# A gate folded into the down weights, three tiles' sums gated early into the residual, and a last quarter normalised on other engines

## The chip, the cores and the metric

The kernel runs on one core of a Trainium2 chip. The metric is the device time of one execution in microseconds (us); for the kernel before it is 829.94 us, the median of three runs (828.57 to 830.37). Engines are named as in the profile: PE is TensorE's matmuls, DVE is VectorE, ACT is ScalarE, POOL is GpSimd, SP is the queue that issues the DMAs.

## What is computed

One layer of a diffusion backbone over 512 tokens of width 1024. Only its last part bears on the change: the gated MLP with a 3x3 depthwise convolution, its down-projection, the gated residual and the last layer norm.

```python
def _conv_ffn(u, rows, cols, w_up, conv_w, conv_b, w_down):
    ...
    a, b = jnp.split(h.reshape(B, L, 2 * D_FF), 2, axis=-1)
    return (jax.nn.gelu(a) * b) @ w_down

def _layer(...):
    ...
    u2 = _modulate(x, sh2, sc2)
    x = _post_norm(DEEPNORM_ALPHA * x + g2 * _conv_ffn(u2, rows, GRID_W, w_up, conv_w, conv_b, w_down),
                   ln2_g, ln2_b)
```

`g2` is a row of 1024 numbers, one for each output column, so it may be multiplied into the sum after the matmuls or into the columns of `w_down` before them. The inner width is 2816, that is 22 tiles of 128 rows of `w_down`.

## The kernel before

**Precision by three matmuls.** Every float32 product is made of three matmuls (`mm3`, lines 92 to 95). A weight tile is split into a rounded half `hi`, which ACT casts (line 88, or 1009 in `spare_split`), and a rest `lo`, which a subtraction makes on DVE or POOL (line 83). Its raw tile (`raw4`, six buffers) comes by one DMA of 512 KB.

**Convolution stage** (lines 1069 to 1097). For each of 44 feature tiles PE makes one PSUM bank (24 matmuls); ACT starts the accumulator and two scaled copies (lines 1078, 1081); POOL adds those two taps (line 996) and makes the `lo` of a later weight tile (line 83); DVE adds six taps (line 998), three for this tile and three for the one before, and a gate product (line 1057) or a `lo` of the activations (line 83). In these loops the order on each engine is as the code says.

**Down stage** (lines 1106 to 1144). The 512 tokens are four blocks, the 1024 output columns two halves, so eight PSUM banks hold all the sums. For each weight tile f (0 to 17 here) all eight banks take three matmuls. `down_prep(f)` loads and splits tile f, with the subtraction on DVE and POOL in turn (`alt`). Only the SP queue's order is fixed there; a scheduler places the instructions of the other engines, and may put them among those of the convolution stage. The last four tiles (18 to 21) are split into kept tiles `lasth`, `lastl`; ACT scales the residual `x1` by ALPHA (line 1141).

**End** (lines 1145 to 1225). For each half of each block the four last tiles are multiplied (`piece`); then DVE multiplies the sum by g2 (line 1152), adds the residual (1153) and takes statistics (1166). The last block's second half is worked in two quarters. The norm is finished on three engines: `finish_pool` (ACT, then two POOL operations), `finish_act` with `centred` (DVE, ACT, one POOL operation), and two DVE operations for the last block. `store` sends each half out.

Of the kernel before, what the change touches and what calls it, by code (L numbers as in the profile page):

```python
# [21 lines left out]
NTB = SEQ // P  # L22
# [23 lines left out]
def layer_kernel(ctx: ExitStack, tc: tile.TileContext, a: dict):  # L46
    nc = tc.nc
    act, dve, pool, pe, dma = nc.scalar, nc.vector, nc.gpsimd, nc.tensor, nc.sync
# [14 lines left out]
    def raw4(shape=(P, D)):  # L63
        return sb.tile(list(shape), F32, tag="raw", bufs=6, name=nm("raw"))
# [38 lines left out]
    part = keep("part", [P, 2, 16])  # L103
# [234 lines left out]
    wh, wl = (sb.tile([P, NF0], F32R, tag=t, bufs=2, name=nm(t)) for t in ("hi", "lo"))  # L338
# [9 lines left out]
    ready = wh, wl  # L348
# [473 lines left out]
    lng = load(row(), a["ln1_g"].broadcast_to([P, D]))  # L822
    lnb = load(row(), a["ln1_b"].broadcast_to([P, D]))
# [3 lines left out]
    x1 = slot(4, [P, NTB, D])  # L827
# [241 lines left out]
    for i in range(2 * NFF):  # L1069
        ps = up_mm(i)  # L1070
# [19 lines left out]
        f = i // 2 - 1  # L1090
# [22 lines left out]
    def down_mm(ps, tb, f, wh, wl, cs, first, last):  # L1113
        ts_ = slice(tb * P, (tb + 1) * P)
        mm3(ps, acts[f // 8][:, f % 8, ts_], acts[3 + f // 8][:, f % 8, ts_], wh[:, cs], wl[:, cs], first, last)

    def down(tb, f, wh, wl):
        for hf, cs in enumerate(HALVES):
            split_end = f == N_FRONT - 1 and hf == 1 and tb == NTB - 1
            down_mm(banks[tb][hf], tb, f, wh, wl, cs, f == 0, split_end)  # L1120

    for w, f in ((down0, 0), (down1, 1)):
        for tb in range(NTB - 1):
            down(tb, f, *w)
    ready = down2
    for w, f in ((down0, 0), (down1, 1)):
        down(NTB - 1, f, *w)
    lasth = slot(1, [P, NFF - N_FRONT, D], F32R)
    lastl = slot(8, [P, NFF - N_FRONT, D], F32R)
    for f in range(2, N_FRONT):  # L1130
        w = ready
        if f + 1 < N_FRONT:
            ready = down_prep(f + 1, alt())
        for tb in range(NTB):
            down(tb, f, *w)
        if f >= N_FRONT - 8 and f % 2 == 0:
            i = (f - N_FRONT + 8) // 2
            raw = load(raw4(), a["w_down"][N_FRONT + i])
            act.copy(lasth[:, i, :], raw)
            sub(dve, lastl[:, i, :], raw, lasth[:, i, :].bitcast(F32))  # L1140
            tc.keep_in_program_order(act.activation(x1[:, i, :], x1[:, i, :], AF.Copy, scale=ALPHA))
    part = banks[NTB - 1][1]
    dve.tensor_tensor(part, part, g2[:, HALVES[1]], ALU.mult)
    dve.tensor_tensor(x1[:, NTB - 1, HALVES[1]], part, x1[:, NTB - 1, HALVES[1]], ALU.add)
    ordered(*ORDT)

    QUARTERS = tuple(slice(i, i + CTX) for i in range(0, D, CTX))
    end = NTB - 1
    st, mean, scale, parts = {}, {}, {}, {}

    def residual(tb, ps, cs):
# [28 lines left out]
    def centred(tb):  # L1180
        for ps, cs in parts[tb]:
            dve.scalar_tensor_tensor(ps, ps, mean[tb], lng[:, cs], ALU.subtract, ALU.mult)

    def finish_pool(tb):
        nmr = small([P, 1])
        dve.tensor_scalar(nmr, mean[tb], scale[tb], -1.0, ALU.mult, ALU.mult)
        for ps, cs in parts[tb]:
            act.activation(x1[:, tb, cs], ps, AF.Identity, bias=nmr, scale=scale[tb])
        for ps, cs in parts[tb]:
# [4 lines left out]
            yield

    def finish_act(tb):
        for ps, cs in parts[tb]:
            z = x1[:, tb, cs]
            act.activation(z, ps, AF.Copy, scale=scale[tb])
            pool.tensor_tensor(z, z, lnb[:, cs], ALU.add)  # L1200
            store(tb, cs)

    for tb in range(end):
        piece(tb, HALVES[0], 0, 2)
        if tb == 1:
            weave(finish_pool(0))
        elif tb:
            finish_act(tb - 1)
        piece(tb, HALVES[1], 1, 2)
        block_scale(tb)  # L1210
        if tb == 1:
            centred(tb)
    piece(end, HALVES[0], 0, 3)
    late = finish_pool(end - 1)
    next(late)
    piece(end, QUARTERS[2], 1, 3)
    piece(end, QUARTERS[3], 2, 3)
    block_scale(end)
    centred(end)
    for i, (ps, cs) in enumerate(parts[end]):  # L1220
        dve.scalar_tensor_tensor(x1[:, end, cs], ps, scale[end], lnb[:, cs], ALU.mult, ALU.add)
        if i != 1:
            store(end, HALVES[min(i, 1)])
        weave(late)
# [75 lines left out]
```

## Time and profile before

| what | us |
|---|---|
| median of three runs | 829.94 |
| the profiled execution | 828.57 |
| its span, first to last instruction | 826.8 |
| PE busy | 801.3 (97%) |
| DVE busy | 537.5 (65%) |
| POOL busy | 401.6 (49%) |
| ACT busy | 365.1 (44%) |

The profiled execution took 828.57 us, of which 1.77 us lie around the span of 826.8 us. Busy shares are means over the whole span; where an engine waits, and for whom, is read from the engines' timelines, in us from the span's start. The convolution stage ends and the down stage begins near 697 us; the last matmul starts at 816.70 us.

### The profile page before, as it was taken

What the parts mean: (1) busy time and instruction counts of PE and PEld (TensorE: products, weight loads), DVE (VectorE), ACT (ScalarE), POOL (GpSimd) and SP (SyncE); (2) the same over time, 40 slices, a digit from 0 to 9 for tenths busy, and PEclk for the clock granted to TensorE, in tenths of its full rate; (3) what the DMA queues carried; (4) which work ended last, traced back from release to release, by engine and by line L of the source; (5) the groups of instructions that cost most, each with busy time, mean ns of one, the idle gap of its engine ahead of it and who ended that gap; (6) DMA issues with size and microseconds to landing.
All of it is one profiled execution on the core that took longest, in us unless ns stands there. A gap on an engine that the chain in (4) does not pass through costs nothing.

```text
span 826.8 us, 10600 instructions
## 1 busy us (share of the span) xinstructions
PE 801.3 (97%) x3865; PEld 668.9 (81%) x3865; DVE 537.5 (65%) x1040; ACT 365.1 (44%) x579; POOL 401.6 (49%) x295
## 2 busy tenths in 40 slices
PE   6989999999999999999999999999999999999995
PEld 4768877888888888888788998888888888888884
DVE  7947789884267773333667579887778877522147
ACT  4644526221454343323325476665566556233101
POOL 3754360021443242104624779988888888321106
PEclk9999999999999999999999999999999999999998
DMA  9950359973220006460504512322232222343002
GB/s 342 405 199 1 140 205 328 324 259 120 75 77 26 1 2 253 133 201 9 205 21 185 192 38 85 117 83 97 103 103 102 83 97 102 102 153 102 1 1 101
DMA packets 34356, 106.94 MB, mean 129 GB/s; under 512 B 4592, under 2 KB 5376, under 8 KB 34304
## 3 DMA queue, kind: packets, MB, share of 16 engines
q1 hardware_dynamic: 34304, 106.27, 36.7%
q8 instruction: 30, 0.49, 0.2%
q14 instruction: 22, 0.18, 0.1%
HBM read 104.14 MB, written 2.11 MB: 129 GB/s over the span
## 4 chain that ended last, share of the span: by engine, by line
PE 87%; DVE 5%; POOL 2%; ACT 2%; issue 2%; DMA 1%; POOLq 0%; SPq 0%; DVEq 0%; ACTq 0%
PE ps L95 26%; PE ps L94 26%; PE ps L93 26%; PE ps L356 3%; PE ps L674 1%; PE ps L644 1%; PE ps L675 1%; POOL S L83 1%; DVE raw L205 1%; DVE S L258 1%; DVE lo L83 1%; PE ps L636 1%; DMA S<-in_x 1%; PE ps L641 1%; POOL lo L83 1%
## 5 line engine op out<-in xcount | busy, mean ns | idle before, releaser
L95 PE MATMUL ps<-S,lo 128*128 128x512 f32 (+1 forms) x560 | 216.4, 388 | 4.2 <-POOL lo L83 3.2
L93 PE MATMUL ps<-S,hi 128*128 128x512 f32 (+1 forms) x560 | 218.2, 390 | 1.0 <-ACT hi L88 1.0
L94 PE MATMUL ps<-S,hi 128*128 128x512 f32 (+1 forms) x560 | 217.1, 388 | 0.0
L83 POOL TENSOR_TENSOR lo<-raw,hi 128x1024 fp32r<-128x1024 f32 (+3 forms) x61 | 141.2, 2317 | 154.6 <-ACT hi L88 152.0
L998 DVE SCALAR_TENSOR_TENSOR t<-ps,convw,t 128x441 f32<-128x441 f32 (+1 forms) x258 | 163.8, 690 | 45.3 <-POOL t L996 45.1
L88 ACT CAST hi<-raw 128x1024 fp32r<-128x1024 f32 (+1 forms) x96 | 99.3, 1035 | 176.1 <-PE ps L95 61.3
L95 PEld LDWEIGHTS ps<-S,lo 128*128 128x128 f32 x560 | 105.6, 189 | 26.9 <-POOL lo L83 4.0
L93 PEld LDWEIGHTS ps<-S,hi 128*128 128x128 f32 x560 | 105.5, 188 | 22.6 <-ACT hi L88 1.5
L94 PEld LDWEIGHTS ps<-S,hi 128*128 128x128 f32 x560 | 105.6, 189 | 21.2
L996 POOL TENSOR_TENSOR t<-t,t 128x448 f32<-128x448 f32 x88 | 101.9, 1158 | 34.4 <-ACT t L1081 31.0
L95 PE MATMUL ps<-S,S 128*128 128x512 f32 (+1 forms) x308 | 112.2, 364 | 0.0
L94 PE MATMUL ps<-S,S 128*128 128x512 f32 (+1 forms) x308 | 112.2, 364 | 0.0
L93 PE MATMUL ps<-S,S 128*128 128x512 f32 (+1 forms) x308 | 111.4, 365 | 0.0
L83 DVE TENSOR_TENSOR lo<-raw,hi 128x1024 fp32r<-128x1024 f32 x37 | 47.2, 1276 | 68.0 <-ACT hi L88 68.0
L94 PE MATMUL ps<-lo,S 128*128 128x512 f32 x208 | 81.0, 390 | 0.0
L95 PE MATMUL ps<-hi,S 128*128 128x512 f32 x208 | 80.8, 389 | 0.0
L93 PE MATMUL ps<-hi,S 128*128 128x512 f32 x208 | 77.2, 391 | 1.6 <-ACT S L546 1.0
L83 POOL TENSOR_TENSOR S<-raw,S 128x1024 fp32r<-128x1024 f32 x21 | 50.6, 2410 | 38.9 <-ACT S L765 23.5
L1078 ACT ACTIVATE t<-ps,convb,convw 128x512 f32<-128x512 f32 x43 | 33.6, 781 | 75.2 <-PE ps L95 75.2
L93 PEld LDWEIGHTS ps<-S,S 128*128 128x128 f32 x308 | 58.1, 189 | 9.2
L94 PEld LDWEIGHTS ps<-S,S 128*128 128x128 f32 x308 | 58.1, 189 | 9.2
L95 PEld LDWEIGHTS ps<-S,S 128*128 128x128 f32 x308 | 58.1, 189 | 9.1
(219 smaller groups left out, 1065.3 us busy)
## 6 DMA issues: line engine op xcount, KB each, us to landing
raw<-in_w_up SPq DMA_DIRECT2D x44, 512.0 KB, 3.3
raw<-in_wada SPq DMA_DIRECT2D x32, 512.0 KB, 5.3
raw<-in_w_down SPq DMA_DIRECT2D x22, 512.0 KB, 3.3
S<-in_wada SPq DMA_DIRECT2D x16, 512.0 KB, 9.6
raw<-in_w_v SPq DMA_DIRECT2D x16, 256.0 KB, 4.5
raw<-in_w_ga SPq DMA_DIRECT2D x8, 512.0 KB, 4.3
raw<-in_w_gb SPq DMA_DIRECT2D x8, 512.0 KB, 3.3
raw<-in_w_br SPq DMA_DIRECT2D x8, 512.0 KB, 4.0
```

The source lines that it names most:

```text
L83: eng.tensor_tensor(out, x, y, ALU.subtract)
L88: act.copy(hi, raw)
L93: pe.matmul(out, lhsT=sh, rhs=mh, start=first, stop=False)
L94: pe.matmul(out, lhsT=sh, rhs=ml, start=False, stop=False)
L95: pe.matmul(out, lhsT=sl, rhs=mh, start=False, stop=last)
L205: dve.scalar_tensor_tensor(out_junk, raw, 1.0, silu_c, ALU.mult, ALU.mult, accum_out=mod[:, j:j + 1])
L258: dve.scalar_tensor_tensor(junk[:, cs], ada_slot(j)[:, cs], 1.0, silu_h[hf], ALU.mult, ALU.mult, accum_out=dst[:, j:j + 1])
L356: pe.matmul(g0[f], lhsT=w[:, f * P:(f + 1) * P], rhs=m[:, kt, :], start=kt == 0 and i == 0, stop=kt == NKT - 1 and i == 2)
L636: pe.matmul(score[h + i][:, ns], lhsT=kT[half_rows, t, ns], rhs=qT[half_rows, t, ns], start=True, stop=True)
L996: pool.tensor_tensor(o, o, i, ALU.add)
L998: dve.scalar_tensor_tensor(o, i, w, o, ALU.mult, ALU.add)
L1078: act.activation(acc, src, AF.Identity, bias=convb[:, i:i + 1], scale=convw[:, i, 4:5])
```

## The change

- Every weight tile of the down stage from f = 3 on, the four kept ones among them, is multiplied by g2 on DVE right after its load (`gated_down`, a product of two tiles of 128x1024 in SBUF); all subtractions of the tiles 3 to 17 are on POOL.
- Tiles 0 to 2 are not multiplied beforehand. Their sums are closed in the eight banks, DVE multiplies each bank by g2 and adds it to ALPHA times the residual (two operations of 128x512 for each bank), and the banks begin anew with tile 3. ACT's four scalings of `x1` are gone.
- At the end DVE no longer multiplies by g2. Blocks 0 to 2 are all finished the same way (DVE, ACT, one POOL operation), and of the last block the last quarter goes over ACT and POOL, the rest over DVE.

```diff
     def down_prep(f, eng):
+        return (split if f % 3 else spare_split)(gated_down(f), (P, D), eng)
+
+    def gated_down(f):
         raw = load(raw4(), a["w_down"][f])
-        return (split if f % 3 else spare_split)(raw, (P, D), eng)
+        dve.tensor_tensor(raw, raw, g2, ALU.mult)
+        return raw
...
+    for blocks, tiles in (((0, 1), (0, 1)), ((0, 1), (2,)), ((2, 3), (0,)), ((2, 3), (1,)), ((2, 3), (2,))):
+        for f in tiles:
+            for tb in blocks:
+                down(tb, f, plain[f], f == N_PLAIN - 1)
+        if tiles == (2,):
+            for tb in blocks:
+                for hf, cs in enumerate(HALVES):
+                    ps = banks[tb][hf]
+                    dve.tensor_tensor(ps, ps, g2[:, cs], ALU.mult)
+                    dve.scalar_tensor_tensor(x1[:, tb, cs], x1[:, tb, cs], ALPHA, ps, ALU.mult, ALU.add)
+    ready = down_prep(N_PLAIN, pool)
...
-            ready = down_prep(f + 1, alt())
+            ready = down_prep(f + 1, pool)
...
-            tc.keep_in_program_order(act.activation(x1[:, i, :], x1[:, i, :], AF.Copy, scale=ALPHA))
-    dve.tensor_tensor(part, part, g2[:, HALVES[1]], ALU.mult)
...
-        dve.tensor_tensor(ps, ps, g2[:, cs], ALU.mult)
-        dve.tensor_tensor(ps, ps, x1[:, tb, cs], ALU.add)
+        dve.tensor_tensor(ps, ps, x1[:, tb, cs], ALU.add)
...
     block_scale(end)
+    centred(end, 0)
+    nmr = small([P, 1])
+    dve.tensor_scalar(nmr, mean[end], scale[end], -1.0, ALU.mult, ALU.mult)
+    ps, cs = parts[end][2]
+    z = x1[:, end, cs]
+    act.activation(z, ps, AF.Identity, bias=nmr, scale=scale[end])
+    pool.tensor_tensor(z, z, lng[:, cs], ALU.mult)
+    pool.tensor_tensor(z, z, lnb[:, cs], ALU.add)
+    scaled(end, 0)
+    store(end, HALVES[0])
+    centred(end, 1)
+    scaled(end, 1)
+    store(end, HALVES[1])
```

The change in the order of instructions is shown at three places. In the names `t_...` are accumulators of the convolution, `ps_...` PSUM banks, `raw_...` raw weight tiles, `row_6082` is g2 and `S_520` is the residual `x1`; line 1029 of the changed kernel is the g2 product, lines 1138 and 1139 are the two operations on a bank.

DVE, in the convolution stage, from the gate product of feature tiles 36 and 37 to the first taps of tile 39 (before):

```order
L1057 TENSOR_TENSOR ps_5825<-ps_5825,t_845_5766 128x512
L998 SCALAR_TENSOR_TENSOR t_852_5813<-ps_5788,convw,t_852_5813 128x8x63
L998 SCALAR_TENSOR_TENSOR t_858_5859<-ps_5834,convw,t_858_5859 128x7x63
L998 SCALAR_TENSOR_TENSOR t_852_5813<-ps_5788,convw,t_852_5813 128x7x63
L998 SCALAR_TENSOR_TENSOR t_858_5859<-ps_5834,convw,t_858_5859 128x7x63
```

and after:

```order
L1062 TENSOR_TENSOR ps_5825<-ps_5825,t_845_5766 128x512
L998 SCALAR_TENSOR_TENSOR t_852_5813<-ps_5788,convw,t_852_5813 128x8x63
L1029 TENSOR_TENSOR raw_6184<-raw_6184,row_6082 128x1024
L998 SCALAR_TENSOR_TENSOR t_858_5859<-ps_5834,convw,t_858_5859 128x7x63
L998 SCALAR_TENSOR_TENSOR t_852_5813<-ps_5788,convw,t_852_5813 128x7x63
L998 SCALAR_TENSOR_TENSOR t_858_5859<-ps_5834,convw,t_858_5859 128x7x63
```

The g2 product of weight tile 3 now stands ahead of the first tap of feature tile 39, where DVE waited for POOL; those of tiles 4 to 7 stand ahead of the first taps of feature tiles 40 to 43 in the same way.

DVE, from the last taps of the convolution into the down stage (before):

```order
L998 SCALAR_TENSOR_TENSOR t_887_6049<-t_886_6047,convw,t_887_6049 128x8x63
L998 SCALAR_TENSOR_TENSOR t_887_6049<-t_886_6047,convw,t_887_6049 128x7x63 x2
L1057 TENSOR_TENSOR t_893_6071<-t_893_6071,t_887_6049 128x512
L83 TENSOR_TENSOR S_603_4032<-t_893_6071,S_600_4029 128x512
L83 TENSOR_TENSOR S_603_4032<-raw_6146,S_600_4029 128x1024
```

and after:

```order
L998 SCALAR_TENSOR_TENSOR t_887_6049<-t_886_6047,convw,t_887_6049 128x8x63
L998 SCALAR_TENSOR_TENSOR t_887_6049<-t_886_6047,convw,t_887_6049 128x7x63
L1029 TENSOR_TENSOR raw_6313<-raw_6313,row_6082 128x1024
L998 SCALAR_TENSOR_TENSOR t_887_6049<-t_886_6047,convw,t_887_6049 128x7x63
L1138 TENSOR_TENSOR ps_6088<-ps_6088,row_6082 128x512
L1138 TENSOR_TENSOR ps_6089<-ps_6089,row_6082 128x512
L1062 TENSOR_TENSOR t_893_6071<-t_893_6071,t_887_6049 128x512
L1138 TENSOR_TENSOR ps_6090<-ps_6090,row_6082 128x512
L1138 TENSOR_TENSOR ps_6091<-ps_6091,row_6082 128x512
L1139 SCALAR_TENSOR_TENSOR S_520_3425<-S_520_3425,ps_6088 128x512
L1139 SCALAR_TENSOR_TENSOR S_520_3425<-S_520_3425,ps_6089 128x512
L1138 TENSOR_TENSOR ps_6092<-ps_6092,row_6082 128x512
```

The g2 product of weight tile 8 and the operations on the banks now stand between the last taps and the last gate product; the first bank (`ps_6088`) is read for the last time by the first row of line 1139. PE writes that bank again with the first matmul of tile 3, in both kernels the 73rd of the down stage, so it follows that row now.

POOL, at the end of the program (before):

```order
L1174 TENSOR_TENSOR sm_6758<-sm_6758,neg_half 128x1
L1191 TENSOR_TENSOR S_520_3425<-S_520_3425,row_6084 128x512
L1192 TENSOR_TENSOR S_520_3425<-S_520_3425,row_6086 128x512
L1174 TENSOR_TENSOR sm_6818<-sm_6818,neg_half 128x1
L1191 TENSOR_TENSOR S_520_3425<-S_520_3425,row_6084 128x512
L1192 TENSOR_TENSOR S_520_3425<-S_520_3425,row_6086 128x512
```

and after:

```order
L1180 TENSOR_TENSOR sm_6780<-sm_6780,neg_half 128x1
L1202 TENSOR_TENSOR S_520_3425<-S_520_3425,row_6086 128x512 x2
L1180 TENSOR_TENSOR sm_6838<-sm_6838,neg_half 128x1
L1213 TENSOR_TENSOR S_520_3425<-S_520_3425,row_6084 128x256
L1214 TENSOR_TENSOR S_520_3425<-S_520_3425,row_6086 128x256
```

Of block 2 POOL has two operations instead of four, both ahead of the last block's square root (the 128x1 row); behind it stand two of 256 columns instead of two of 512.

## Rows read from the trace of the kernel before

**Rows 1.** The page: chain that ended last by engine; then a DMA issue, us to landing

```profile
PE 87%; DVE 5%; POOL 2%; ACT 2%; issue 2%; DMA 1%; POOLq 0%; SPq 0%; DVEq 0%; ACTq 0%
...
raw<-in_w_down SPq DMA_DIRECT2D x22, 512.0 KB, 3.3
```

**Rows 2.** PE's timeline: start, us, engine, line, operation; two places of the down stage

```profile
713.31 1.98 PE L93 MATMUL ps<-S,S 128*128 128x512 f32 x8
...
816.70 0.28 PE L95 MATMUL ps<-S,S 128*128 128x256 f32 x1
```

**Rows 3.** DVE's timeline, end of the convolution stage, and one later row

```profile
679.30 3.08 DVE L998 SCALAR_TENSOR_TENSOR t<-ps,convw,t 128x441 f32<-128x441 f32 x5 [1.06 <-POOL t L996]
...
682.89 0.73 DVE L998 SCALAR_TENSOR_TENSOR t<-ps,convw,t 128x504 f32<-128x504 f32 x1
...
695.66 3.08 DVE L998 SCALAR_TENSOR_TENSOR t<-ps,convw,t 128x441 f32<-128x441 f32 x5 [1.18 <-POOL t L996]
...
701.86 2.79 DVE L998 SCALAR_TENSOR_TENSOR t<-t,convw,t 128x441 f32<-128x441 f32 x1 [1.88 <-POOL t L996]
...
707.59 2.16 DVE L998 SCALAR_TENSOR_TENSOR t<-t,convw,t 128x504 f32<-128x504 f32 x3
...
726.89 1.23 DVE L83 TENSOR_TENSOR S<-raw,S 128x1024 fp32r<-128x1024 f32 x1 [0.15 <-ACT S L1139]
```

**Rows 4.** POOL's timeline, near 105 us

```profile
105.02 2.15 POOL L480 TENSOR_TENSOR t<-t,t 128x512 f32<-128x512 f32 x1
107.25 2.16 POOL L83 TENSOR_TENSOR t<-t,t 128x512 f32<-128x512 f32 x1
```

**Rows 5.** DVE's timeline, same stretch

```profile
105.96 2.30 DVE L83 TENSOR_TENSOR lo<-raw,hi 128x1024 fp32r<-128x1024 f32 x1
```

**Rows 6.** POOL's timeline, end of the convolution stage

```profile
679.20 2.43 POOL L83 TENSOR_TENSOR lo<-raw,hi 128x1024 fp32r<-128x1024 f32 x1
...
701.79 2.39 POOL L83 TENSOR_TENSOR lo<-raw,hi 128x1024 fp32r<-128x1024 f32 x1
```

**Rows 7.** Busy us in a stretch: PE, PEld, DVE, ACT, POOL; clock, DMA, GB/s

```profile
600.00:700.00 100.00, 100.00 (x443) 82.81 (x442) 79.93 (x130) 62.52 (x95) 84.92 (x56) 1.00 0.29 98
```

**Rows 8.** SP's timeline: the load of down weight tile 3

```profile
676.26 0.33 SPq L98 DMA_DIRECT2D raw<-in_w_down  x1
```

**Rows 9.** ACT's timeline: first cast of the down stage; two finishing operations

```profile
711.11 1.05 ACT L1009 CAST S<-raw 128x1024 fp32r<-128x1024 f32 x1
...
816.69 1.45 ACT L1188 ACTIVATE S<-ps,sm,sm 128x512 f32<-128x512 f32 x2 [3.17 <-DVE sm L1186]
```

**Rows 10.** DVE's timeline, end of the program

```profile
811.27 0.70 DVE L1166 BATCH_NORM_STATS2 t<-ps 128x6 f32<-128x512 f32 x1
811.88 0.68 DVE L1152 TENSOR_TENSOR ps<-ps,row 128x512 f32<-128x512 f32 x1
...
817.84 0.42 DVE L1152 TENSOR_TENSOR ps<-ps,row 128x256 f32<-128x256 f32 x1
...
819.50 0.15 DVE L1173 TENSOR_SCALAR sm<-sm 128x1 f32<-128x1 f32 x1
```

**Rows 11.** POOL's timeline, end of the program

```profile
820.10 0.55 POOL L1174 TENSOR_TENSOR sm<-sm,neg_half 128x1 f32<-128x1 f32 x1
...
821.96 1.26 POOL L1192 TENSOR_TENSOR S<-S,row 128x512 f32<-128x512 f32 x1
```

**Rows 12.** SP's timeline: the last store

```profile
823.68 0.38 SPq L1178 DMA_DIRECT2D out_x<-S  x1
```

**Rows 13.** Busy us in stretches, columns as in rows 7: a PE gap, and the end

```profile
52.00:56.00 4.00, 1.25 (x5) 0.51 (x4) 1.23 (x2) 3.23 (x5) 2.63 (x2) 1.00 0.01 2
...
57.00:60.00 3.00, 3.00 (x9) 2.32 (x8) 0.00 (x0) 0.00 (x0) 1.08 (x1) 0.50 0.71 231
60.00:61.00 1.00, 1.00 (x5) 0.77 (x5) 0.00 (x0) 0.00 (x0) 0.00 (x0) 0.88 0.78 315
...
821.00:822.00 1.00, 0.00 (x0) 0.00 (x0) 1.00 (x3) 0.00 (x0) 0.92 (x2) 0.71 0.69 262
```

More of the change, by code (lines that the diff above doesn't have):

```diff
@@ L1115, in down_mm, with down @@
         mm3(ps, acts[f // 8][:, f % 8, ts_], acts[3 + f // 8][:, f % 8, ts_], wh[:, cs], wl[:, cs], first, last)
-    def down(tb, f, wh, wl):
+    def down(tb, f, w, last):
         for hf, cs in enumerate(HALVES):
             split_end = f == N_FRONT - 1 and hf == 1 and tb == NTB - 1
[L1120 to L1127, printed above, removed]
+            down_mm(banks[tb][hf], tb, f, *w, cs, f in (0, N_PLAIN), last or split_end)
@@ new lines, in layer_kernel @@
+    N_PLAIN = 3
+    plain = (down0, down1, down2)
+    for blocks, tiles in (((0, 1), (0, 1)), ((0, 1), (2,)), ((2, 3), (0,)), ((2, 3), (1,)), ((2, 3), (2,))):
[8 more added lines that the diff above has]
+                    dve.scalar_tensor_tensor(x1[:, tb, cs], x1[:, tb, cs], ALPHA, ps, ALU.mult, ALU.add)
@@ L1128, in layer_kernel @@
+    ready = down_prep(N_PLAIN, pool)
     lasth = slot(1, [P, NFF - N_FRONT, D], F32R)
     lastl = slot(8, [P, NFF - N_FRONT, D], F32R)
-    for f in range(2, N_FRONT):
+    for f in range(N_PLAIN, N_FRONT):
         w = ready
         if f + 1 < N_FRONT:
-            ready = down_prep(f + 1, alt())
+            ready = down_prep(f + 1, pool)
         for tb in range(NTB):
-            down(tb, f, *w)
+            down(tb, f, w, False)
         if f >= N_FRONT - 8 and f % 2 == 0:
             i = (f - N_FRONT + 8) // 2
-            raw = load(raw4(), a["w_down"][N_FRONT + i])
+            raw = gated_down(N_FRONT + i)
@@ L1139, in layer_kernel @@
             act.copy(lasth[:, i, :], raw)
             sub(dve, lastl[:, i, :], raw, lasth[:, i, :].bitcast(F32))
-            tc.keep_in_program_order(act.activation(x1[:, i, :], x1[:, i, :], AF.Copy, scale=ALPHA))
     part = banks[NTB - 1][1]
-    dve.tensor_tensor(part, part, g2[:, HALVES[1]], ALU.mult)
     dve.tensor_tensor(x1[:, NTB - 1, HALVES[1]], part, x1[:, NTB - 1, HALVES[1]], ALU.add)
     ordered(*ORDT)
-    QUARTERS = tuple(slice(i, i + CTX) for i in range(0, D, CTX))
     end = NTB - 1
@@ L1149, in layer_kernel @@
     st, mean, scale, parts = {}, {}, {}, {}
-    def residual(tb, ps, cs):
-        dve.tensor_tensor(ps, ps, g2[:, cs], ALU.mult)
-        dve.tensor_tensor(ps, ps, x1[:, tb, cs], ALU.add)
     def piece(tb, cs, n, of):
-        apart = tb == end and cs.start >= SEQ
+        apart = cs.stop - cs.start == CTX
         ps = bank()[:, 0:CTX] if apart else banks[tb][cs.start // SEQ]
@@ L1161, in piece @@
                     apart and f == N_FRONT, f == NFF - 1)
-        residual(tb, ps, cs)
+        dve.tensor_tensor(ps, ps, x1[:, tb, cs], ALU.add)
         if n == 0:
@@ L1178, in store, with centred @@
         dma.dma_start(a["out"][tb * P:(tb + 1) * P, cs], x1[:, tb, cs])
[L1180 to L1189, printed above, removed]
+    def centred(tb, n):
+        ps, cs = parts[tb][n]
+        dve.scalar_tensor_tensor(ps, ps, mean[tb], lng[:, cs], ALU.subtract, ALU.mult)
@@ L1190, in finish_pool, with scaled @@
+    def scaled(tb, n):
+        ps, cs = parts[tb][n]
+        dve.scalar_tensor_tensor(x1[:, tb, cs], ps, scale[tb], lnb[:, cs], ALU.mult, ALU.add)
+    for tb in range(end):
+        for hf, cs in enumerate(HALVES):
+            piece(tb, cs, hf, 2)
+        block_scale(tb)
+        for hf, cs in enumerate(HALVES):
+            centred(tb, hf)
             z = x1[:, tb, cs]
-            pool.tensor_tensor(z, z, lng[:, cs], ALU.mult)
+            act.activation(z, parts[tb][hf][0], AF.Copy, scale=scale[tb])
@@ L1192, in finish_pool @@
             pool.tensor_tensor(z, z, lnb[:, cs], ALU.add)
             store(tb, cs)
[L1194 to L1217, printed above, removed]
-    block_scale(end)
[L1219 to L1224, printed above, removed]
+    for n, cs in enumerate((HALVES[0], slice(SEQ, SEQ + CTX), slice(SEQ + CTX, D))):
+        piece(end, cs, n, 3)
```

## The prediction

> **What bounds the kernel now.** The chain that ended last comes first: 87% of it is PE [rows 1]. The convolution stage gives PE's pace: three feature tiles of 24 matmuls lie between the first taps at 679.30 and 695.66 [rows 3], so 5.45 us for a tile and 0.227 us for a matmul. The first three weight tiles of the down stage are 72 matmuls; they end where the eight of tile 3 begin, at 713.31 [rows 2], so the stage begins near 713.31 - 72 x 0.227 = 697.0 and PE goes through it without a gap. Next the two engines that the change loads, at the end of the convolution stage: DVE's rows carry waits of 1.06 to 1.88 us for POOL [rows 3], and POOL is busy 84.92 of 100 us [rows 7]. Last the tail: the last matmul ends at 816.70 + 0.28 = 816.98 [rows 2] and the span at 826.8, 9.82 us in which DVE, POOL and the stores decide. So time is won only behind 816.98, and lost wherever PE is made to wait.
>
> **A row that decides the rest.** At 105.96 a DVE operation on two SBUF tiles took 2.30 us [rows 5]; alone one of this size takes 1.23 [rows 3]. POOL's operation ended at 107.17, and DVE's 1.09 later; POOL's next, begun at 107.25, ended at 109.41 [rows 4], 1.15 after DVE's. The two engines took turns: each waited until the other's running instruction was over, but for about 0.15 us. The tap at 701.86, also with two SBUF operands, took 2.79 beside POOL's 701.79 to 704.18 [rows 3, 6]; the five taps at 679.30 read a PSUM bank and took 3.08 in all beside POOL's subtraction [rows 3, 6]. The products by g2 have two SBUF operands; the operations on the banks have one. The Trainium skill (GPSIMD Engine Reference, section "Key points") says that GpSimd shares its SBUF interfaces with VectorE and contends with instructions of two SBUF inputs; how long either waits it doesn't say. The rows agree on the kind and show a full turn; were it a sharing at half rate each, the held products would end some 0.7 to 0.9 us sooner and the sum below would be about +4.5 instead of +6.2.
>
> **Products in the convolution stage.** Five products of 1.23 us stand where DVE waited 1.06 to 1.88, so by length they nearly fit. The first doesn't: its raw tile is issued at 676.26 [rows 8] and lands 3.3 later [rows 1], at 679.56, when the wait was already over (679.30) and POOL has been subtracting since 679.20 until 681.63 [rows 6]. It ends at 681.63 + 1.09 = 682.7: the taps are 3.4 us late. From there DVE needs 4.32 us for a tile's taps (679.30 to 682.89 + 0.73 [rows 3]) and 1.23 for a product, 5.4 with overlaps, just PE's pace; each product meets POOL again. An extra wait of 0 to 2.4 us each is possible; POOL's subtractions, themselves pushed back, leave about 0.35 (the product of tile 4 comes at 686.9, POOL is done at 687.3). After three more tiles the lag is 3.4 + 3 x 0.35 = 4.4, so tile 42's taps begin at 700.1 instead of 695.66. Then the gate product, two SBUF operands too, meets POOL's subtraction of 701.79, now 0.8 later, and loses 1.7. The next product adds 1.2 with POOL idle. In the old kernel DVE lost 1.88 waiting and 2.1 held in this place [rows 3], so at the first tap of tile 43 the lag is 4.4 + 1.7 + 1.2 - 4.0 = 3.3. PE just misses it: the last bank that these taps set free is read by the third tap behind 704.65 (701.86 + 2.79), at 0.6 us apart until 706.4 before and 709.7 now, and PE asks for it as the 58th matmul, at 697.0 + 57 x 0.227 = 709.9.
>
> **Draining the banks.** The last but one tap ended at 709.75 - 0.7 [rows 3] and now ends at 712.4. Next on DVE is the product of tile 8. PE is through with tile 0's weights after 60 matmuls, at 710.8; ACT's cast of 1.05 [rows 9] into their place ends at 711.9, and POOL subtracts for tile 3 until about 714.6. The product is held and ends at 715.7. Six operations follow at 0.62 us apart (811.27 to 811.88 [rows 10]): a tap, two bank products, the last gate product, two bank products; then the residual addition of the first bank, 0.70. That is 715.7 + 6 x 0.62 + 0.70 = 720.1. PE wants this bank for tile 3 at 713.3 and waits **6.8 us**. If the product came before POOL, the tap behind it would be held instead: 5.7; if a tap delayed POOL's subtraction by its own 0.7, 7.5. Queued behind the waiting matmul is all the rest of PE's work, so none of this is won back.
>
> **After the wait.** The second bank comes 0.6 later; further on DVE's last subtraction is held by POOL's for tile 5, which costs PE some 0.6 at the fourth bank and 0.3 at the fifth: 1.3 in all. The clock matters too. After 52 to 56 us, in which PE worked 1.25 us, the granted clock stood at 0.50, that is 1.2 GHz, with 9 matmuls in 57 to 60, and was back in the slice of 60 to 61; in the silence after the last matmul, at 816.98, it fell in the slice of 821 to 822 [rows 13]. I therefore expect PE to come out of a wait of 6.8 us at half speed, and to stay there 3 to 4 us as it did from 57 to 60: 1.5 to 2.1 us of work, in which part of the 1.3 hides. I take **1.9** for both, 1.3 to 2.5 as bounds.
>
> **Edits at nothing.** ACT loses four scalings; it waits for others in this stage. POOL makes every subtraction of the tiles 3 to 17, 2.40 of each 5.45 us, and DVE a product of 1.23 ahead of it; PE's 5.45 us on a tile hide both, with six raw buffers ahead. Without that cover product, cast and subtraction (1.23 + 1.05 + 2.40, and a hold of up to 2.4) would exceed a tile by up to 1.6 us.
>
> **The tail.** Without its g2 product DVE has 4.7 us of work for a block against PE's 5.45, so it reaches the last quarter on time and not 0.86 late (817.84 [rows 10] against 816.98). From T, the last matmul's end: statistics 1.36 (817.84 to 819.65 less one operation of 0.45), the root 0.55 on a POOL that no longer works on block 2 [rows 11], 0.2 for a product of scalars, ACT's quarter 0.4 to 0.75 (half to all of 1.45/2 [rows 9]), two POOL operations of 256 columns at 0.63 to 0.75 (from 1.26 for 512 [rows 11]), so T + 4.2; the last store then takes 3.12 to the end, as from 823.68 [rows 12]. That is T + 7.3 instead of T + 9.8: **-2.5**, at least -2.0.
>
> **Sum.** 6.8 + 1.9 - 2.5 = **+6.2 us**. The profiled execution of 828.57 would become 834.8; the median of the three runs is 1.37 above it, so I forecast 829.94 + 6.2 = 836.1. With the bounds of the terms (5.7 to 7.5, 1.3 to 2.5, -2.0 to -2.6) this case runs from 834.3 to 838.
>
> **Rivals.** (A) *The products find the port free*, a win. Place: the six products of tiles 3 to 8. Were none held, the first would end at 680.8, the lag would be 1.8 at tile 42, and -1.0 at the last taps, since the old 2.1 hold of 701.86 would go too; the first bank would be free at 713.8, PE would wait 0.5 to 1.1, and with -2.5 the time is 828.3. It decides from the point where each product falls between two POOL instructions; POOL's 85% [rows 7] speaks against it. (B) *Half of it*: the holds come, but the wait at the first bank is only 2 to 3 us, since POOL's subtraction for tile 3 falls behind the last tap, and the clock holds. Then the tail pays for the wait: 829.5 to 831. That needs DVE three microseconds earlier than the rows give. (C) *The tail gives nothing*: the change doesn't do what it says there, because ACT and POOL form a chain as long as the old one. Then 836.1 + 2.5 = 838.6. Against it stand 4.2 us in known pieces.
>
> **How the numbers follow.** Forecast 0.72, A 0.12, B 0.08, C 0.08. A measurement of this kernel tells about 0.2%, or 1.7 us, from no change. Faster: A, 0.12. Within: B, 0.08. Slower: forecast and C, 0.80. The range of 829.2 to 839.0 holds B, nearly all of the forecast and about half of C: 0.08 + 0.69 + 0.04, 8 in 10.
>
> **What would show it.** In the changed profile: products of line 1029 longer than 1.23 in 679 to 717, up to 3.5; the taps of tile 39 near 682.7; one PE gap of some 7 us at 713 that DVE's line 1139 ends; the granted clock at half right behind it; between the last matmul and the end of the span 7.3 us. Wrong would be: products at 1.23 beside a busy POOL, or a first residual addition that ends before 715.

## The result

| kernel | median, us | range |
|---|---|---|
| before, in the same runs | 830.15 | 828.57 to 830.52 |
| changed | 835.97 | 833.92 to 836.28 |

The changed kernel takes 1.0069 times as long (95% interval 1.0048 to 1.0089), some 5.7 us more on 829.94. The forecast was 836.1, slower.

One caution for reading the two traces side by side. DVE's tap of 504 columns that stands ahead of the first product began at 677.50 in the trace of before and here at 679.01 (the first row of the view below). In the timeline of before it is

```profile
677.50 0.73 DVE L998 SCALAR_TENSOR_TENSOR t<-ps,convw,t 128x504 f32<-128x504 f32 x1
```

The same row lay at 677.25 to 677.60 in eight of the fourteen traces of this document and at 678.94 to 679.69 in the other six, though ahead of it all fourteen have the same 3240 matmuls and 942 operations on DVE, 526 on ACT and 260 on POOL (261 in pairs_late_lo). The granted clock tells the two groups apart: summed over the slices ahead of that tap it stood at 0.50 for 3.4 us in each of the eight and for 6.8 us in each of the six. One stretch at 0.50 lies between 140 and 160 us in the changed kernel's trace and not in that of before (first before, then changed; busy us, columns as in rows 7):

```profile
140.00:160.00 20.00, 19.50 (x86) 16.05 (x86) 18.65 (x40) 9.20 (x20) 0.00 (x0) 1.00 0.85 294
```

```profile
140.00:160.00 20.00, 19.50 (x79) 15.87 (x79) 18.64 (x40) 9.20 (x20) 0.00 (x0) 0.91 0.87 293
```

Half of those further 3.4 us, 1.7, is the work that PE lost by them (an estimate), so most of the gap between the groups. Why the clock stood low longer in some executions is open. A traced execution can thus be up to 2.4 us late before it comes to the change, whatever the change is, and I count everything from that tap. From it to the start of the last matmul the kernel before took 816.70 - 677.50 = 139.20 us [rows 2]; the changed one takes 826.28 - 679.01 = 147.27, which is **8.07 more**.

DVE in the changed kernel, from its timeline (start, us, engine, line, operation, tiles, shape, count, and in brackets the idle time before it with what ended it); it answers to [rows 3]. Line 1029 is the g2 product, 1062 the gate product, 1138 and 1139 the two operations on a bank:

```profile
679.01 0.73 DVE L998 SCALAR_TENSOR_TENSOR t<-ps,convw,t 128x504 f32<-128x504 f32 x1
681.51 2.67 DVE L1029 TENSOR_TENSOR raw<-raw,row 128x1024 f32<-128x1024 f32 x1 [1.77 <-DMA raw<-in_w_down]
684.11 3.07 DVE L998 SCALAR_TENSOR_TENSOR t<-ps,convw,t 128x441 f32<-128x441 f32 x5
...
688.35 1.54 DVE L1029 TENSOR_TENSOR raw<-raw,row 128x1024 f32<-128x1024 f32 x1
...
704.23 2.27 DVE L1062 TENSOR_TENSOR t<-t,t 128x512 f32<-128x512 f32 x1
...
711.80 1.44 DVE L998 SCALAR_TENSOR_TENSOR t<-t,convw,t 128x504 f32<-128x504 f32 x2
713.16 1.22 DVE L1029 TENSOR_TENSOR raw<-raw,row 128x1024 f32<-128x1024 f32 x1
714.30 2.77 DVE L998 SCALAR_TENSOR_TENSOR t<-t,convw,t 128x441 f32<-128x441 f32 x1
716.99 1.28 DVE L1138 TENSOR_TENSOR ps<-ps,row 128x512 f32<-128x512 f32 x2
...
719.99 1.27 DVE L1139 SCALAR_TENSOR_TENSOR S<-S,ps 128x512 f32<-128x512 f32 x2
...
722.98 2.83 DVE L83 TENSOR_TENSOR S<-t,S 128x512 fp32r<-128x512 f32 x1
```

POOL beside it; it answers to [rows 6]:

```profile
680.72 2.40 POOL L83 TENSOR_TENSOR lo<-raw,hi 128x1024 fp32r<-128x1024 f32 x1
...
713.42 3.17 POOL L83 TENSOR_TENSOR S<-raw,S 128x1024 fp32r<-128x1024 f32 x1 [7.48 <-ACT S L1009]
720.54 4.72 POOL L83 TENSOR_TENSOR lo<-raw,hi 128x1024 fp32r<-128x1024 f32 x2 [3.95 <-ACT hi L88]
```

PE there, the group of these matmuls on the page (busy us, mean ns, idle before and its releaser), and the granted clock in slices of 1 us (the value ahead of the DMA share; the counts are the instructions of PE, PEld, DVE, ACT, POOL that touch a slice):

```profile
714.59 0.39 PE L95 MATMUL ps<-hi,S 128*128 128x512 f32 x1
720.81 1.30 PE L93 MATMUL ps<-S,S 128*128 128x512 f32 x2 [5.83 <-DVE S L1139]
...
722.34 0.63 PE L95 MATMUL ps<-S,S 128*128 128x512 f32 x1
722.76 0.63 PE L94 MATMUL ps<-S,S 128*128 128x512 f32 x1
...
826.28 0.28 PE L95 MATMUL ps<-S,S 128*128 128x256 f32 x1
```

```profile
L93 PE MATMUL ps<-S,S 128*128 128x512 f32 (+1 forms) x308 | 112.1, 368 | 5.8 <-DVE S L1139 5.8
```

```profile
717.00:718.00 1.00, 0.00 (x0) 0.00 (x0) 1.00 (x3) 0.00 (x0) 0.00 (x0) 1.00 0.51 82
718.00:719.00 1.00, 0.00 (x0) 0.00 (x0) 1.00 (x3) 0.10 (x1) 0.00 (x0) 0.55 0.90 332
...
721.00:722.00 1.00, 1.00 (x3) 0.65 (x4) 1.00 (x3) 0.41 (x1) 1.00 (x1) 0.50 0.00 0
724.00:725.00 1.00, 1.00 (x4) 0.76 (x3) 1.00 (x1) 0.00 (x0) 1.00 (x1) 0.53 0.75 279
725.00:726.00 1.00, 1.00 (x6) 0.83 (x5) 1.00 (x2) 0.00 (x0) 0.27 (x1) 1.00 0.53 213
```

Four things are to be seen. The tap behind the product at 713.16 was held to 2.77 us, since POOL's subtraction began at 713.42. The first bank was free after the first of two residual additions, at 719.99 + 0.67 = 720.66. PE was silent for 5.83 us until then. Afterwards it ran at half clock: the matmuls start 0.42 us apart (722.34 and 722.76), where the prediction's pace is 0.227. Of the 8.07 us, 5.83 are the wait, and 2.24 were lost behind it. The tail, from the end of the last matmul (826.28 + 0.28) to the end of the span (834.0), is 7.44 instead of 9.82 [rows 2]: 2.38 gained. Net 8.07 - 2.38 = 5.7, as the medians say.

### The profile page after: what moved, and what is told of

It reads as the page before. It is cut to its first block, busy times and chain, and to the rows that moved or that the text cites. A ratio compares the mean times of both kernels' runs of the same rounds, so it can differ in the third digit from the quotient of the medians.

```text
span 834.0 us, 10643 instructions
## 1 busy us (share of the span) xinstructions
PE 806.2 (97%) x3865; PEld 672.6 (81%) x3865; DVE 566.5 (68%) x1058; ACT 361.4 (43%) x576; POOL 418.5 (50%) x301
## 4 chain that ended last, share of the span: by engine, by line
PE 83%; DVE 8%; issue 2%; ACT 2%; POOL 2%; DMA 1%; SPq 0%; POOLq 0%; DVEq 0%; ACTq 0%
PE ps L95 25%; PE ps L93 25%; PE ps L94 25%; PE ps L356 3%; DVE t L998 2%; DVE raw L1029 1%; POOL S L83 1%; PE ps L675 1%; PE ps L644 1%; PE ps L674 1%; DVE raw L205 1%; DVE lo L83 1%; PE ps L298 1%; PE ps L636 1%; PE ps L641 1%
## 5 line engine op out<-in xcount | busy, mean ns | idle before, releaser
L83 POOL TENSOR_TENSOR lo<-raw,hi 128x1024 fp32r<-128x1024 f32 (+2 forms) x66 | 153.5, 2328 | 132.7 <-ACT hi L88 129.5
L83 POOL TENSOR_TENSOR S<-raw,S 128x1024 fp32r<-128x1024 f32 x24 | 58.7, 2449 | 55.2 <-ACT S L1009 29.4
L83 DVE TENSOR_TENSOR lo<-raw,hi 128x1024 fp32r<-128x1024 f32 x32 | 40.2, 1257 | 31.7 <-ACT hi L88 31.6
```

The costliest lines, as they stand in the source:

```text
L83: eng.tensor_tensor(out, x, y, ALU.subtract)
```

## Experiments

Two figures serve for all of them. **Stretch**: from the start of the tap of 504 columns ahead of the first taps of feature tile 39 to the start of the last matmul. **First bank**: from the same tap to the end of the first addition on line 1139, when PE may restart on it (line numbers shift by a few in the other kernels). PE asks for it some 35.9 us after the tap. In the kernel before, its next matmul starts 713.31 [rows 2] - 677.50 = 35.81 after it; in the changed one its last matmul ends 720.81 - 5.83 - 679.01 = 35.97 after it. The two differ because matmuls overlap, each being 0.39 us long and starting 0.227 behind the last. "Behind" is the stretch less 139.20 and less the waits; some 0.16 us of it for each wait is only this overlap.

Five kernels (pairs_late_lo, no_last_late_lo, no_first_late_lo, late_lo and late_lo_filled) were executed once, so their trace is compared and not their time. The stretch is steady enough for that: before, late_drain and the two kernels of the tail have 139.18 to 139.20. For the first wait of one_operand and of no_last_late_lo the trace names a cast of ACT as the end; PE started 0.14 us behind DVE's addition there, as in the others, so I count it as DVE's.

| kernel | first bank | PE's waits | stretch | behind |
|---|---|---|---|---|
| before | - | 0 | 139.20 | 0 |
| changed | 41.65 | 5.83 | 147.27 | 2.24 |
| one_operand | 37.04 | 1.22 + 2.83 | 146.32 | 3.07 |
| no_products | 34.84 | 3.31 | 144.34 | 1.83 |
| no_products_late_lo | 34.86 | 0.51 | 140.38 | 0.67 |
| copies_late_lo | 34.85 | 0.50 | 140.34 | 0.64 |
| pairs_late_lo | 36.58 | 0.75 + 1.24 | 143.65 | 2.46 |
| no_last_late_lo | 38.14 | 2.31 + 0.64 | 145.62 | 3.47 |
| no_first_late_lo | 41.47 | 5.64 | 148.13 | 3.29 |
| late_lo | 41.65 | 5.83 | 147.07 | 2.04 |
| late_lo_filled | 41.69 | 0.44 + 0.23, 5.44 filled | 146.31 | 1.00 |
| late_drain | - | 0 | 139.20 | 0 |

### Is it the products' work, or their second SBUF operand?

**one_operand:**

```diff
-        dve.tensor_tensor(raw, raw, g2, ALU.mult)
+        if f < 9:
+            dve.tensor_scalar(raw, raw, 1.0, 0.0, ALU.mult, ALU.add)
+        else:
+            dve.tensor_tensor(raw, raw, g2, ALU.mult)
```

> The products of weight tiles 3 to 8 (those made before the banks are drained) become an operation on the same 128x1024 elements with one SBUF operand, a multiplication by 1; the gate is then missing from these six tiles, the rest is as in the changed kernel. Theory (turns at the SBUF port): the operation takes about 1.25 us wherever it falls, the taps of tile 39 come some 1.6 us sooner than with the product, PE waits for the first bank 0.5 to 2 us instead of 5.8. The last lo of the activations, two SBUF operands, may still meet POOL's subtraction for tile 3, for up to 2.5 us at the second bank. Time 830.5 to 833. Rival 1 (DVE is simply given too much work before the drain): six operations of the same length change nothing, first wait 5 to 6 us, time 835.5 to 836.5. Rival 2 (the drain itself is what PE waits for): the same, 835.5 to 836.5.

It took 1.0061 times the time of before (1.0038 to 1.0084), about 835.0. That is above the theory's range and just below the rivals'. Two of the substitutes on DVE, and POOL at the first of them:

```profile
682.26 1.99 DVE L1030 TENSOR_SCALAR raw<-raw 128x1024 f32<-128x1024 f32 x1 [1.93 <-DMA raw<-in_w_down]
...
712.16 0.69 DVE L1030 TENSOR_SCALAR raw<-raw 128x1024 f32<-128x1024 f32 x1
716.54 2.28 DVE L83 TENSOR_TENSOR S<-t,S 128x512 fp32r<-128x512 f32 x1
```

```profile
681.30 2.39 POOL L83 TENSOR_TENSOR lo<-raw,hi 128x1024 fp32r<-128x1024 f32 x1
```

The substitute was no clean one. Alone it takes 0.69 us, not 1.25, and beside POOL 1.22 to 2.24: this operation with one SBUF operand waits for POOL too. So the taps of tile 39 came only 0.5 us sooner, where the theory had 1.6. The Trainium skill (SBUF — State Buffer, section "Who interferes with whom") says just that, that a scalar operation may run in a mode that uses the shared ports, and that whoever of the two engines starts first keeps them for the whole instruction. The rows agree: the operation begun at 682.26 ended at 684.25, 0.56 us behind POOL's subtraction (683.69), where a sharing at half rate would have ended it near 682.26 + 2 x 0.69 = 683.6 (an estimate). The first bank still came 4.6 us sooner, and the first wait of 1.22 is the theory's. The second bank, held by the `lo` at 716.54, cost 2.83, which the expectation had named with up to 2.5. What it left out is the price behind the waits: after 1.22 + 2.83 PE ran at half clock as it did after 5.83, and lost another 3.07.

**no_products**, and **no_products_late_lo**, which also moves DVE's last `lo` of the activations behind the drain:

```diff
-        dve.tensor_tensor(raw, raw, g2, ALU.mult)
+        if f > 8:
+            dve.tensor_tensor(raw, raw, g2, ALU.mult)
```

```diff
-    act_out_lo(NFF - 1)
...
-                    dve.scalar_tensor_tensor(x1[:, tb, cs], x1[:, tb, cs], ALPHA, ps, ALU.mult, ALU.add)
+                    one = dve.scalar_tensor_tensor(x1[:, tb, cs], x1[:, tb, cs], ALPHA, ps, ALU.mult, ALU.add)
+    with tc.issue_after(one.ins):
+        act_out_lo(NFF - 1)
```

Behind the loop `one` is the last addition of the drain.

> The products of weight tiles 3 to 8 are left out (the gate is missing from these six tiles), the drain and the tail are as in the changed kernel. Theory (turns): DVE is through with the taps as early as in the kernel before and PE finds the first bank drained; at the second bank it may wait 2 to 3 us, where the last lo of the activations meets POOL's subtraction for tile 3. Time 829 to 831.5. Rival 1 (work): the same first wait of 0 to 0.5 us and none at the second bank, 827.5 to 828.5. Rival 2 (the drain): 16 operations at 0.63 us ahead of PE cost nearly the full wait, 4 to 6 us, time 834 to 836.

> As no_products (products of the tiles 3 to 8 left out, so the gate is missing from these), and DVE's last lo of the activations (two SBUF operands, 2.90 us there beside POOL's subtraction, between the first and the second drained bank) is queued behind the whole drain. In no_products PE waited 3.31 us at the second bank and came out at half clock. Theory (it was the hold of this one operation, not the 16 drain operations): waits of 0.4 to 1.2 us in all, no half clock, the tail's 2.4 us remain, time 828 to 829.2. Rival (the 16 operations are too much for DVE there): a wait of 2.5 us or more at the second or third bank, 831 to 832.5.

no_products: 1.0030 (1.0016 to 1.0045), about 832.4, a microsecond above the theory's range; PE came out of the wait at half clock here too, and the term behind it is 1.83. In the table its first bank is on time (34.84). DVE and PE at the second bank:

```profile
712.09 2.90 DVE L83 TENSOR_TENSOR S<-t,S 128x512 fp32r<-128x512 f32 x1
```

```profile
716.84 0.80 PE L93 MATMUL ps<-S,S 128*128 128x512 f32 x1 [3.31 <-DVE S L1140]
```

no_products_late_lo: 0.9986 (0.9974 to 0.9997), about 828.8, as the theory had it. The rival that the 16 drain operations are too much there falls: with that one operation out of the way they cost 1.18 us in all.

**copies_late_lo** and **pairs_late_lo** are no_products_late_lo with other work in the five places that the products had in the convolution stage; the sixth product (tile 8) has no substitute. In copies_late_lo it is two copies from PSUM to SBUF:

```diff
+    def copies(bank_):
+        for cs in (slice(0, SEQ), slice(SEQ, D)):
+            dve.tensor_copy(work[:, cs], bank_)
+        yield
...
+        if i >= 39:
+            gens.insert(1, copies(srcs[i - 1]))
```

In pairs_late_lo the body of `copies` is one product in SBUF:

```diff
+        dve.tensor_tensor(work, work, work, ALU.mult)
+        yield
```

> As no_products_late_lo, but in the place of each of the five products of the convolution stage (ahead of the first tap of the feature tiles 39 to 43) DVE copies a PSUM bank of 128x512 twice, some 1.3 us, into a tile that nobody reads: the products' work without their second SBUF operand and without their load. Theory (turns): the copies fit into DVE's waits for POOL, DVE is at most 0.5 us later at the drain, time within 1 us of no_products_late_lo, 828 to 830. Rival 1 (DVE is given too much work there): the first bank comes 2.5 us later or more, and the time is 831.5 or above.

> As copies_late_lo, but in the place of the two copies stands one product of a 128x1024 SBUF tile with itself (zeros, nobody reads it): the five products' second SBUF operand without their load and without the sixth product (tile 8; the gate is missing from the tiles 3 to 8). From the last tap of 504 columns before feature tile 39 to the last matmul no_products_late_lo took 140.38 us and copies_late_lo 140.34, the kernel before 139.20, late_lo 147.07. Theory (turns at the port alone delay DVE): operations of 1.5 to 2.3 us, POOL's subtractions pushed back, 141 to 143. Rival (what delays DVE is that the first product waits for its load): 140.3 to 140.6.

DVE's second insertion, of copies and then of pairs, and POOL's subtraction in pairs, then PE's waits, in copies and in pairs:

```profile
685.02 1.28 DVE L1051 COPY row<-ps 128x512 f32<-128x512 f32 x2
```

```profile
684.69 1.53 DVE L1051 TENSOR_TENSOR row<-row 128x1024 f32<-128x1024 f32 x1
```

```profile
685.10 3.40 POOL L83 TENSOR_TENSOR lo<-raw,hi 128x1024 fp32r<-128x1024 f32 x1
```

```profile
715.64 1.09 PE L93 MATMUL ps<-S,S 128*128 128x512 f32 x2 [0.50 <-DVE S L1148]
```

```profile
714.25 0.47 PE L93 MATMUL ps<-S,S 128*128 128x512 f32 x1 [0.75 <-DVE S L1148]
715.95 1.39 PE L93 MATMUL ps<-S,S 128*128 128x512 f32 x2 [1.24 <-DVE S L1148]
```

copies_late_lo: 0.9985 (0.9974 to 0.9995), and every figure of the table as without them. Five times 1.28 us of DVE work at this place cost nothing; rival 1, the amount of work, falls for these five. pairs_late_lo, of nearly the same length and without any load, brings the first bank 1.73 us later and the stretch to 143.65, beyond both forecasts, with DVE at 1.53 and POOL's subtraction at 3.40 for 2.42. So work that reads both operands from SBUF has a price where work of the same length that reads PSUM has none. The size was under-rated: 1.99 us are PE's waits, and 2.46 were lost behind them, with PE at half clock.

### Which of the products?

**no_first_late_lo** and **no_last_late_lo** leave one product out of late_lo (below):

```diff
-        dve.tensor_tensor(raw, raw, g2, ALU.mult)
+        if f != 3:
+            dve.tensor_tensor(raw, raw, g2, ALU.mult)
```

In no_last_late_lo the condition is `f != 8`.

> As late_lo, with the product of tile 3 alone left out (the one that waits 1.60 us for its load; the gate is missing from tile 3). Same stretch as above, late_lo 147.07. Theory A (the late first product gives DVE the lag that all later steps carry): 3.4 us less lag at tile 39, PE waits 2 to 3 us less, 143 to 145. Theory B (the holds of the later products and of the gate product would bring DVE to the same lag, and the last product decides): 146.3 to 147.

> As late_lo, with the product of tile 8 alone left out (the one among the last two taps; the gate is missing from tile 8). Late_lo: 147.07, with the tap behind this product held to 2.77 us by POOL's subtraction for tile 3. Theory B (this product brings the end of the taps into POOL's subtraction): the drain begins 2.5 to 4 us sooner, PE waits 2 to 4 us instead of 5.83, 143 to 144. Theory A (its own 1.2 us, the lag from the first product stays): 145 to 146.

DVE of no_first at feature tile 40, and of no_last at the last taps:

```profile
679.69 0.73 DVE L998 SCALAR_TENSOR_TENSOR t<-ps,convw,t 128x504 f32<-128x504 f32 x1
681.49 3.08 DVE L998 SCALAR_TENSOR_TENSOR t<-ps,convw,t 128x441 f32<-128x441 f32 x5 [1.06 <-POOL t L996]
...
687.25 3.13 DVE L1030 TENSOR_TENSOR raw<-raw,row 128x1024 f32<-128x1024 f32 x1 [1.44 <-DMA raw<-in_w_down]
```

```profile
710.07 2.16 DVE L998 SCALAR_TENSOR_TENSOR t<-t,convw,t 128x504 f32<-128x504 f32 x3
...
714.74 0.68 DVE L1139 SCALAR_TENSOR_TENSOR S<-S,ps 128x512 f32<-128x512 f32 x1
```

Without the first product the taps of tile 39 begin 1.80 us after the tap of 504 columns (681.49 - 679.69) instead of 5.1, so 3.3 less lag; but the next product waits for its own load and then 3.13 us for POOL, and the first bank is only 0.18 sooner. Theory A falls in its form "the late first product sets the lag": whichever product comes first is late. The stretch, 148.13, is above theory B's range too, by what was lost behind the wait (3.29 where late_lo lost 2.04). Without the product of tile 8 the taps are through before POOL begins, the first bank is 3.5 us sooner and the waits are 2.95: theory B's place and size. Yet the stretch, 145.62, is in A's range, since 3.47 us were lost behind the waits instead of 2.04: PE worked at 0.50 for some 6.1 us, against 3.7 in late_lo.

### What does the half clock cost?

**late_lo** is the changed kernel with the `lo` moved as above; **late_lo_filled** lets PE work through the wait:

```diff
+                    for k in range(9):
+                        down_mm(banks[tb][1], tb, f, *plain[f], HALVES[1], False, k == 8)
```

That is tile 2 into the last bank, eight times too often.

> The changed kernel with DVE's last lo of the activations queued behind the whole drain. It is the ground for the next run. Both theories: PE waits 5.5 to 6.5 us at the first bank, the granted clock then stands at 0.5 for 4 us or more, and from the wait's end PE loses another 1.5 to 2.2 us.

> As late_lo, but PE multiplies tile 2 eight further times into the last bank (24 matmuls, 5.44 us; the sum of this bank is then too large) before it asks for the first drained bank, so that it works through most of the wait. Theory (the half clock behind the wait costs time of its own): the granted clock stays at 1.00, PE waits 0.4 to 1.5 us at the first bank and about 1 us at the following ones, and its last matmul comes 0.6 to 1.2 us earlier than in late_lo. Rival (DVE's drain sets PE's pace behind the wait, the clock costs nothing): the last matmul within 0.3 us of late_lo.

late_lo did as expected: a wait of 5.83, the clock at 0.50 for 6.8 us, and 2.04 lost behind the wait. PE and the clock in late_lo_filled:

```profile
719.25 0.47 PE L93 MATMUL ps<-S,S 128*128 128x512 f32 x1 [0.44 <-DVE S L1143]
722.15 0.51 PE L93 MATMUL ps<-S,S 128*128 128x512 f32 x1 [0.23 <-DVE S L1143]
```

```profile
720.00:721.00 1.00, 0.91 (x5) 0.42 (x3) 1.00 (x3) 0.00 (x0) 1.00 (x1) 1.00 0.00 0
721.00:722.00 1.00, 0.92 (x3) 0.43 (x3) 1.00 (x2) 0.00 (x0) 1.00 (x2) 1.00 0.03 8
```

The clock stayed at 1.00 and the stretch fell from 147.07 to 146.31, 0.76 less, within the 0.6 to 1.2 expected. The rest does not come back: beside the filled 5.44 us there are 0.67 of waits and 1.00 behind them, in which PE goes at the pace of DVE's drain. So the clock cost something, but less than the whole term behind the wait: in late_lo half of PE's 3.7 us of work at 0.50 would be 1.8 us (an estimate), and without the half clock the drain still takes part of it.

### Where does the tail's gain come from?

**late_drain_old_finish** has no g2 product at the end, but the finishing of before; **new_finish_only** is before with the changed kernel's finishing alone.

> The kernel late_drain with the finishing of the kernel before (block 0 and 2 over ACT and two POOL operations, block 1 over DVE, ACT and one POOL operation, the last block all on DVE), still without the g2 product at the end. It splits the tail's 2.4 us. Theory: the product taken off DVE gives about 0.9 (DVE was 0.86 late at the last quarter), the other finishing about 1.5: time 828.7 to 829.4. Rival 1: the product gives it all, 827.3 to 828.2 as late_drain. Rival 2: the finishing gives it all, 829.7 to 830.3.

> The kernel before with nothing but the changed kernel's finishing of the norm (blocks 0 to 2 over DVE, ACT and one POOL operation, the last quarter over ACT and POOL), the g2 product still at the end on DVE. Theory (the finishing pays only where DVE is rid of the g2 product; with it DVE has 5.4 to 6.1 us for a block and falls behind PE): the end 0 to 1 us later than before, time 829.9 to 831. Rival (the finishing gives its 1.5 us by itself): 828.2 to 828.8.

From the end of the last matmul to the end of the span: 9.82 us before, 827.6 - 818.76 = 8.84 in late_drain_old_finish, 827.4 - 817.07 = 10.33 in new_finish_only, 824.1 - 816.73 = 7.37 in late_drain, which has both. The ratios say the same: 0.9992 (0.9980 to 1.0005), 1.0014 (1.0005 to 1.0024), 0.9972. So the product off DVE gives 1.0; the other finishing loses 0.5 by itself and gives 1.5 where DVE is rid of the product. DVE's last additions to the last quarter show why, first new_finish_only (last matmul's end 817.07), then late_drain (816.73):

```profile
820.03 0.43 DVE L1153 TENSOR_TENSOR ps<-ps,S 128x256 f32<-128x256 f32 x1
```

```profile
816.83 0.43 DVE L1192 TENSOR_TENSOR ps<-ps,S 128x256 f32<-128x256 f32 x1 [0.34 <-PE ps L95]
```

In the one DVE is 3 us behind PE, in the other it waits for it.

### The drain at another place

**late_drain** drains after weight tile 8; tiles 0 to 8 are not multiplied, and only 9 to 21 are.

```diff
-    N_PLAIN = 3
...
+    N_PLAIN = 9
...
+    L = N_PLAIN - 3
...
+    for blocks in ((0, 1), (2, 3)):
+        for f in range(L, N_PLAIN):
...
+            for tb in blocks:
+                down(tb, f, tiles[f], f == N_PLAIN - 1)
...
+        for tb in blocks:
+            for hf, cs in enumerate(HALVES):
+                ps = banks[tb][hf]
+                dve.tensor_tensor(ps, ps, g2[:, cs], ALU.mult)
+                dve.scalar_tensor_tensor(x1[:, tb, cs], x1[:, tb, cs], ALPHA, ps, ALU.mult, ALU.add)
```

> The banks are drained after weight tile 8 instead of tile 2: tiles 0 to 8 not multiplied (subtractions on DVE and POOL in turn, as in the kernel before), tiles 6 to 8 worked for blocks 0 and 1 first and then for blocks 2 and 3, products only for tiles 9 to 21. Drain and products then lie in the down stage, where DVE has 5.45 us for a tile. Theory (the loss is only the place where products and drain meet the end of the convolution): no PE wait over 0.5 us, the tail keeps its 2.4 us, time 827.3 to 828.2, faster than both kernels. Rival (the drain and its products cost PE time wherever they are): waits of 2 us or more at tile 9, 830 or above.

827.05 us against 828.69 in the same runs, ratio 0.9972 (0.9960 to 0.9985), which is 827.6 on 829.94: faster than both kernels, as expected. PE has no wait behind the convolution, and the drain runs at its own length:

```profile
742.09 1.87 DVE L1170 SCALAR_TENSOR_TENSOR S<-S,ps 128x512 f32<-128x512 f32 x3
743.88 1.25 DVE L1029 TENSOR_TENSOR raw<-raw,row 128x1024 f32<-128x1024 f32 x1
745.05 2.48 DVE L1169 TENSOR_TENSOR ps<-ps,row 128x512 f32<-128x512 f32 x4
```

The place is not all that differs: the products of tiles 3 to 8 are gone here and not moved, since these tiles' sums are multiplied in the banks. How much each has can be read from no_products_late_lo, which drains at the early place without these products and with the `lo` out of the way (and so leaves the gate out of six tiles): its stretch is 140.38. Of the 8.07 us, some 6.9 go with the products and the `lo`, and 1.2 with the early place of the drain itself.

## Why the prediction was right, step by step

- **Turns at the port** (right). The six products took 2.67, 1.54, 1.56, 1.54, 1.21 and 1.22 us. The one begun at 681.51 beside POOL's subtraction of 680.72 to 683.12 ended at 684.18, 1.06 behind it; at half rate each it would have ended near 683.5 (an estimate). The other way round, POOL's subtraction begun 0.26 us behind the product of tile 8 took 3.17 for 2.40. That these turns cost PE time is shown by copies_late_lo against pairs_late_lo.
- **The first product** came at 681.51 and let the taps of tile 39 go at 684.11, which is 682.6 on the clock of before's trace (1.51 earlier); 682.7 was forecast. But as the cause of what follows this step was wrong: no_first_late_lo took it away and the first bank came no sooner. The lag is set by whichever products come later, above all by the last.
- **The lag in between** was somewhat over-rated: the last but one tap ended at 713.24, on before's clock 711.7 where 712.4 was forecast.
- **Draining the banks.** Of the three orders considered the product of tile 8 came first, by 0.26 us (713.16 and 713.42), and the tap behind it was held. The bound for that order was 5.7, and 5.83 was measured; the term taken, 6.8, was the one for the other order. This is the mis-sized term. Taken out one after the other in the experiments, from 34.85 us without products to 41.65 the first bank's delay of 6.8 splits into 1.7 for the five operations on SBUF alone (pairs), 1.6 for what the real five have more (their loads and a gate product held 2.27; these two were not told apart), and 3.5 for the product of tile 8.
- **After the wait**: 2.24 for 1.9, inside the bounds. The trace shows 4.1 us at half clock with work on PE, where the forecast had 3 to 4. That is in part luck: the clock stood at 0.50 for 6.8 us, about twice as long as in the stretch that the forecast was taken from, but 2.7 of them lay inside the wait.
- **The tail**: 2.38 for 2.5; the two shares were not forecast apart, and the second exists only with the first.
- **Edits at nothing** (right): no PE wait follows in the changed kernel after the one at 720.81, so the subtractions on POOL and the products did not hold PE there.
- **Sum**: 5.83 + 2.24 - 2.38 = 5.7 for 6.2. The sum was right by its path, and its closeness has luck in it: the wait was 1.0 too long, the other two terms made up for half of that, and the order at the last product was decided by 0.26 us. Rival A (port free) was near in its arithmetic, not in its condition: with copies for five of the products and the last `lo` out of the way the time is some 828.7, where it had 828.3. Rival B's half wait and rival C's idle tail did not come.

## What to carry to other kernels

Before putting work into an engine's waits, look at what the other engine does there: five operations of 1.28 us that read PSUM were free, and five of nearly the same length that read both operands from SBUF beside a busy POOL were not. When a wait in front of PE is short, its price is not the wait alone; ask too for how long the clock is down afterwards. A block of work that is right but in a crowded place may be moved to where the same engines have slack: here the later drain, which also does without six of the products, turned a loss of 5.7 us into a gain of 2.3.

## What was not expected of the hardware

- The half clock's length does not follow the length of the wait. By the slices the clock was at 0.50 for 6.8 us in the changed kernel (718.1 to 724.9), in one_operand, late_lo, no_first_late_lo and no_last_late_lo, after waits of 2.95 to 5.83 us, and for 3.4 us in no_products (3.31) and pairs_late_lo (0.75 + 1.24). What it cost went, in two traces, with how much of it lay inside the wait. In late_lo the clock fell at 715.9, 3.2 us before PE restarted, and 2.04 were lost; in no_first_late_lo, after nearly the same wait, it fell at 720.7, 0.6 us before, and 3.29 were lost. Half of PE's work at 0.50 would be 1.8 and 3.1 us (estimates from 3.7 and 6.2 us). The clock of no_first_late_lo:

```profile
720.00:721.00 1.00, 0.00 (x0) 0.00 (x0) 1.00 (x2) 1.00 (x3) 0.00 (x0) 0.86 0.00 0
721.00:722.00 1.00, 0.69 (x2) 0.48 (x3) 1.00 (x3) 0.91 (x1) 0.96 (x1) 0.50 0.00 0
...
727.00:728.00 1.00, 1.00 (x4) 0.73 (x4) 1.00 (x2) 0.00 (x0) 0.00 (x0) 0.72 0.92 324
```

- In pairs_late_lo the clock fell after two waits of 0.75 and 1.24 us with one matmul between them; in no_products_late_lo, after one of 0.51, it stayed at 1.00.
- A DVE multiplication of 128x1024 by a constant takes 0.69 us with POOL idle, about half of a product of two tiles (1.21), and up to 2.24 beside POOL.
